# Two of the four value projections of a mixer layer computed in seven half-sized products, as the other two already are, and placed earlier

## The chip, the cores and the metric

The kernel runs on one core of a Trainium2 chip. The core has TensorE (PE: matmuls, with its weight loads listed as PEld), VectorE (DVE), ScalarE (ACT), GpSimd (POOL), SyncE (SP), and 16 DMA engines that move data between DRAM and the on-chip memory SBUF; matmuls write to PSUM, whose banks the other engines empty. The metric is the device time of one execution in microseconds (us); lower is better.

## What is computed

One decoder layer in fp32 on x of 512 x 1024. One projection of x gives queries, keys and values of three attention branches and three gates; the branches are projected, gated and summed, and an MLP follows.

```
proj = x @ w_in
(da_q, da_k, da_v, sb_q, sb_k, sb_v, dl_q, dl_k, dl_v, gates) = split(proj)
o_da = diff_attention(da_q, da_k, da_v, ...)            # 4 heads
o_sb = stick_breaking_attention(sb_q, sb_k, sb_v)       # 8 heads
o_dl = dilated_attention(dl_q, dl_k, dl_v, rel_bias)    # 3 groups x 4 heads
g = sigmoid(gates)
merged = g0 * (o_da @ w_branch_da) + g1 * (o_sb @ w_branch_sb) + g2 * (o_dl @ w_branch_dil)
x = layer_norm(alpha * x + merged @ w_out)
x = layer_norm(alpha * x + square(relu(x @ w_up)) @ w_down + sigmoid(x @ w_ple_gate) * (p @ w_ple))
```

The change concerns the value columns: da_v (512 columns) and dl_v (three groups of 512 columns, dl_v0, dl_v1, dl_v2), each a product of x (512 x 1024) with a 1024 x 512 weight.

## The kernel before

**Products.** Each fp32 product is made of three products of the type fp32r: a number is split into a high part (rounded) and a low part (the rest), and high x high, high x low and low x high are summed in PSUM. A weight chunk is 128 x 1024 (0.5 MB). SyncE loads it into `raw` (a ring of 6), ScalarE casts the high part `wh` (line 264), VectorE subtracts to get the low part `wl` (line 266, "the split"); `wh` and `wl` are rings of 5.

**Items.** The work of TensorE outside the heads is a list of items, each of which fills a PSUM bank and is evacuated. A "T" item makes 128 columns of queries or keys transposed, in 24 matmuls of one chunk. A "V" makes four items (`v_items`, matmuls at 602 to 604, evacuated by the copy at 617), one for each 128 rows of x, 24 matmuls each, all four reading the same four chunks. `value_pair` makes two values together: x and the two weights are treated as 2 x 2 blocks, and seven products of half the depth and half the rows replace eight (Strassen's scheme in Winograd's form). That gives 14 half items of 12 matmuls (570 to 572), two for each of the products 1, 2, 7, 6, 4, 5, 3. Each product reads two chunks of 128 x 1024, so there are 14 chunk splits. Products 1, 2 and 4 read weights as they are; 5 and 6 read sums of weight blocks, `vsum`, made in DRAM; 7 and 3 take the chunk loaded for product 1 or 6 and let GpSimd add one more weight block to it in SBUF after the split (`then_add`, line 178). Products 7, 6, 4 and 5 use sums of blocks of x, the forms u7, u6, u4, u5, made by `mixer_forms` on VectorE and ScalarE (696 to 718); the gates use the same forms later. A product's halves are evacuated by ScalarE copies (577) and by VectorE additions (580 to 590). The halves of a pair alternate between PSUM's mm banks (2) and at banks (6); products 5 and 3 add up in at banks. The attention heads use the at banks too. Values of the dilated branch go to DRAM (`values`, 534) and are read back in the heads' order (`dl_vh`, 542).

**Order.** The list: first items of the stick-breaking branch, then the dilated queries and keys (T), with dl_v0's four items among them, then da_v's four items, then the pair of dl_v1 and dl_v2 (item 31 is its first; `pair_at` holds that number), then groups, gates and the rest. The program is written in the list's order: `pump` issues splits ahead of their items, and with each item the heads in flight advance by one step (8 stick-breaking, 4 dilated, 4 differential heads); a scheduler then arranges the instructions by priority and readiness. The forms start at `pair_at - 6`, the tables of the differential heads at `pair_at + 20`, and from `pair_at + 12` on the splits are ordered behind the heads' last instructions.

**Sums.** The sums of weight blocks (`vsum`, `qsum`, `msum`, `bsum`, `gsum`, `usum`, `dsum`) are made by DMAs that GpSimd issues: a plain copy (1233) or one that adds (1231). They are doled out: each item adds its rate times its size to a credit, and each whole unit of credit issues the next step of a fixed list. Each step waits for an earlier split, so that the steps are spread over the stream. An item without a rate of its own takes it from a table by its number (945).

Of the kernel before, what the change touches and what calls it, by code (L numbers as in the profile page):

```python
# [10 lines left out]
F32 = mybir.dt.float32  # L11
# [24 lines left out]
def main_order():  # L36


    o = [("T", "sb_q", 0), ("T", "sb_k", 0), ("T", "sb_q", 1), ("T", "sb_k", 1), ("V", "sb_v", 0)]
    for j in (2, 3):  # L40
        o += [("T", "sb_q", j), ("T", "sb_k", j)]
    for h in range(2):
        for g in range(3):
            o += [("T", "dl_q", 4 * g + h), ("T", "dl_k", 4 * g + h)]
            if h == 1 and g == 0:
                o += [("V", "dl_v", g)]
    o += [("V", "da_v", 0), ("V", "dl_v", 1), ("V", "dl_v", 2)]
    pairs = [(("dl_q", 4 * g + h), ("dl_k", 4 * g + h)) for h in (2, 3) for g in range(3)]
    groups = [("G", tuple(pairs[2 * i:2 * i + 2]), i) for i in range(3)]
    o += groups[:2]  # L50
    for d in range(4):
        if d == 2:
            o += groups[2:]
        o += [("T", "da_q", d), ("T", "da_k", d)]
    return o


def trunk(tc, a, out):
    nc = tc.nc
    es = ExitStack()  # L60
    with es:
# [23 lines left out]
        def at_bank():  # L85
            return psum.tile([P, 512], F32, name=nm("at"), tag="at", bufs=6)
# [95 lines left out]
        def chained(cs, p, kp, w, sums):  # L182

            if p in (7, 3):
                return then_add(cs[{7: 1, 3: 6}[p]][kp], w[{7: 2, 3: 1}[p]])
            return chunk(sums[p == 6] if p in (5, 6) else w[{1: 0, 2: 1, 4: 3}[p]], 1024)
# [168 lines left out]
        def group_items(gi, pairs):  # L355
# [21 lines left out]
            def add(ps, need, free, run, ev, bank):  # L377
                for p in ps:
                    at = {5: 0, 6: 1, 7: 2, 3: 3}.get(p)
                    cs[p] = [chunk(w[{1: 0, 2: 1, 4: 3}[p]] if at is None else qsum[gi][at], 1024)]  # L380
                item([c for p in free for c in cs[p]], lambda b: run(), lambda b: ev(),
                     need=[c for p in need for c in cs[p]], bank=bank)
                items[-1]["rate"] = 0.5

            def put(*args):
                with tc.high_priority():
# [121 lines left out]
                T["sb_q", 0], T["sb_k", 0] = evac_sides(*ps, scale["sb_q"])  # L508
            item(parts + [cs[k][0] for k in (1, 3, 5, 7)], mm, ev, bank=lambda: (at_bank(), at_bank()))

        vsum = [[dram.tile([P, 1024], F32, name=f"vsum{m}_{i}") for i in range(2)] for m in range(2)]
        def load_xr():

            r = {}
# [27 lines left out]
                nc.gpsimd.dma_start(t.rearrange("p (c d) -> p c d", c=4), rows)  # L542
            return [t.rearrange("p (c d) -> p c d", c=4) for t in ts]

        def value_pair(nv):


            pair_at.append(len(items))
            cs, s, x = {}, {}, {}
            w = [[a["wv"][nv + n, 2 * h + kp].rearrange("p k n -> p (k n)") for n in range(2) for h in range(2)]  # L550
                 for kp in range(2)]

            for p in (1, 2, 7, 6, 4, 5, 3):
                for r in range(2):
                    if not r:
                        cs[p] = [chained(cs, p, kp, w[kp], vsum[kp]) for kp in range(2)]

                    def bank(p=p, r=r):
                        if p == 5:
                            x[r] = at_bank()  # L560
                        return x[r] if p in (5, 3) else at_bank() if r else mm_bank()

                    def mm(ps, p=p, r=r):
                        for k in range(4):
                            c = cs[p][k // 2]
                            n = slice(k % 2 * 512, k % 2 * 512 + 512)
                            q = slice(r * P, r * P + P)
                            h, lo = [t[:, q] for t in xf[p][k]]
                            go, end = k == 0 and p != 3, k == 3 and p != 5
                            nc.tensor.matmul(ps, h, c["h"][:, n], start=go, stop=False, skip_group_check=True)  # L570
                            nc.tensor.matmul(ps, h, c["l"][:, n], start=False, stop=False, skip_group_check=True)
                            nc.tensor.matmul(ps, lo, c["h"][:, n], start=False, stop=end, skip_group_check=True)

                    def ev(ps, p=p, r=r):
                        if p in (1, 7):
                            s[p, r] = slot("dl_v")
                            nc.scalar.copy(s[p, r], ps)
                        elif p == 2:
                            t = slot("dl_v")
                            nc.vector.tensor_add(t, s[1, r], ps)  # L580
                            keep(1, r, t)
                        elif p == 6:
                            nc.vector.tensor_add(s[1, r], s[1, r], ps)
                            nc.vector.tensor_add(s[7, r], s[7, r], s[1, r])
                        elif p == 3:
                            nc.vector.tensor_add(s[1, r], s[1, r], ps)
                            keep(1, 2 + r, s[1, r])
                        else:
                            t = slot("dl_v") if p == 4 else s[7, r]
                            nc.vector.scalar_tensor_tensor(t, s[7, r], -1.0, ps, op0=OP.mult, op1=OP.subtract)  # L590
                            keep(2, r + 2 * (p == 5), t)
                    item(cs[p] if r else [], mm, ev, need=cs[p], bank=bank, size=0.5)
                    items[-1]["rate"] = 0.5

        def v_items(nv, name, g):
            cs = [chunk(a["wv"][nv, c].rearrange("p k n -> p (k n)"), 1024) for c in range(4)]
# [29 lines left out]
            for tt in range(4):  # L626
# [14 lines left out]
                def ev(ps, tt=tt):  # L641
                    if name != "sb_v" or tt:
# [1 line left out]
                first = name == "sb_v" and tt < 2  # L644
                item(cs if tt == 3 else [], mm, ev, need=cs[2 * tt:2 * tt + 2] if first else cs,
                     bank=((lambda: two[0]) if tt else at_bank) if first else None)
                items[-1]["rate"] = 0.0 if name == "da_v" and not tt else 2.4

        nt, nv = 2, 0
        pair_at = []  # L650
# [2 lines left out]
        for kind, name, j in order[2:]:  # L653
            if kind == "T":
                t_item(nt, name, j)
                nt += 1
            elif kind == "G":
                group_items(j, name)
            else:
                if name != "dl_v" or j == 0:  # L660
                    v_items(nv, name, j)
                elif j == 1:
                    value_pair(nv)
                nv += 1


# [53 lines left out]
        def seven(forms, operand, bank_of, done):  # L720

            cs = {}
            for p in (1, 2, 7, 6, 4, 5, 3):
                for r in range(2):
# [20 lines left out]
                    if p == 5:  # L745
                        bank_of.get("sums", set()).add(len(items))
                    item(cs[p] if r else [], mm, ev, need=cs[p], bank=bank, size=0.5)
                    items[-1]["rate"] = 1.0

        msum = [[[dram.tile([P, 1024], F32, name=f"msum{n}_{m}_{i}") for i in range(2)] for m in range(2)]  # L750
                for n in range(3)]
# [190 lines left out]
            item([], mm, ev, size=0.08)  # L942

        for j, it in enumerate(items):
            it.setdefault("rate", 3.0 if j < 12 else 2.8 if j < 24 else 0.0 if j < 27 else 2.1 if j < 46 else 2.7)

        gate_alone(0, 1)
        gate_alone(1, 2)
# [247 lines left out]
        def sum_steps():  # L1196
# [32 lines left out]
            def issue(o, i, plus):  # L1229
                if plus:  # L1230
                    i = nc.gpsimd.dma_start(o, i, accum_op=OP.add, max_dma_last_dim=4096)  # L1231
                else:
# [3 lines left out]
                    mybir.DependencyClass.Sync, mybir.DependencyReason.DATA), reason="spread over the main stream")  # L1236

            w = a["wv"].rearrange("g c p k n -> g c p (k n)")
            todo = deque(two_steps(vsum[m], [w[3 + i // 2, i % 2 * 2 + m] for i in range(4)], True)
                         for m in range(2))  # L1240
            todo.extend(up_steps(qsum[m], a["wq"][m]) for m in range(3))
            for n in range(3):
                todo.extend(two_steps(msum[n][m], a["wgm"][n, m]) for m in range(2))
# [905 lines left out]
                except StopIteration:  # L2149
                    pending.remove(g)  # L2150

        DA_TABS = pair_at[0] + 20
        sum_steps_ = sum_steps()
        credit = 0.0
        forms_at = pair_at[0] - 6
# [2 lines left out]
        for n, it in enumerate(items):  # L2158
# [27 lines left out]
            pump(freed, {1: 3, 3: 0, 4: 0, ple_at: 0, ple_at + 1: 0}.get(n, 1 if n < 10 else 2))  # L2186
            if n == 8:
                tie.clear()
            tied[0] = pair_at[0] + 12 <= n < gated_at
            if n == gated_at:  # L2190
                tie.clear()
            if n == 4:
# [165 lines left out]
```

## Time and profile before

| | |
|---|---|
| median of 3 runs | 1031.75 us (1031.61 to 1031.76) |
| the profiled execution's own time | 1031.94 us |
| its span in the trace | 1030.2 us (1.74 us lie around it) |
| instructions | 15628 |
| DMA | 270.74 MB in 79533 packets |
| granted TensorE clock, mean | 0.998 |

Times in the profile are of one execution. A row of a group reads: line, engine, operation, tile written <- tiles read, shape, count; then either the busy time in all and the mean of one in ns, and the idle time before them with its releaser, or the shortest, median and longest duration in ns with the first and last start in us. "x8" is a count. Matmuls are pipelined, so one lasts longer than the distance to the next.

### The profile page before, as it was taken

The page shows a single profiled execution, that of the slowest core. Times are in us where ns is not written, and L with a number is a line of the kernel's source. Part 1 is how long each engine was busy: PE and PEld are TensorE (multiplying, and loading weights), DVE is VectorE, ACT ScalarE, POOL GpSimd, SP SyncE. Part 2 cuts the span into 40 slices and gives each one's busy share as a digit, 9 for nine tenths or more (in the row PEclk, how much of TensorE's full clock was granted, in tenths as well). Part 3 has the DMA queues.
Part 4 walks back from the last instruction along what each step waited for, and adds up shares of the span by engine and source line. Part 5 has one row for each costly group of instructions (what it writes and reads, how often), then busy time and mean ns, then how long its engine had stood idle before and what let it go on. Part 6 is the DMA issues. An engine that isn't in the chain of part 4 may idle for free.

```text
span 1030.2 us, 15628 instructions
## 1 busy us (share of the span) xinstructions
PE 1019.7 (99%) x5650; PEld 883.5 (86%) x5650; DVE 782.5 (76%) x1393; ACT 607.3 (59%) x1045; POOL 205.0 (20%) x307
## 2 busy tenths in 40 slices
PE   9999999999999999999999999999999999999997
PEld 6888888888998898888888888889999899899886
DVE  6888656677656876886878885798768777777975
ACT  7566556665444565656654743776666556556651
POOL 0323421121323122111122140211121111110001
PEclk9999999999999999999999999999999999999999
DMA  8999997778999889778999995699999999988522
GB/s 311 293 287 296 263 292 248 214 209 220 287 342 258 248 266 247 167 232 206 359 315 266 333 340 170 136 251 350 332 306 315 307 342 335 297 256 277 177 80 82
DMA packets 79533, 270.74 MB, mean 263 GB/s; under 512 B 9720, under 2 KB 12552, under 8 KB 79456
## 3 DMA queue, kind: packets, MB, share of 16 engines
q0 software_dynamic: 36624, 130.89, 50.1%
q1 hardware_dynamic: 42256, 137.95, 36.6%
q8 instruction: 44, 0.72, 0.3%
q10 hardware_dynamic: 576, 0.92, 0.2%
q14 instruction: 33, 0.27, 0.1%
HBM read 262.35 MB, written 112.22 MB: 364 GB/s over the span
## 4 chain that ended last, share of the span: by engine, by line
PE 91%; DVE 4%; ACT 2%; DMA 2%; issue 1%; DVEq 0%; ACTq 0%
PE mm L89 9%; PE mm L90 9%; PE mm L91 9%; PE at L1414 4%; PE at L1415 4%; PE at L1416 4%; PE at L737 2%; PE at L735 2%; PE at L736 2%; PE mm L604 2%; PE mm L602 2%; PE mm L603 2%; PE at L91 2%; PE at L90 2%; PE at L89 2%; DMA raw<-in_wb_dram 2%
## 5 line engine op out<-in xcount | busy, mean ns | idle before, releaser
L266 DVE TENSOR_TENSOR wl<-raw,wh 128x1024 fp32r<-128x1024 f32 x268 | 322.7, 1214 | 113.1 <-ACT wh L264 112.0
L264 ACT CAST wh<-raw 128x1024 fp32r<-128x1024 f32 x268 | 277.6, 1042 | 208.0 <-PE mm L90 102.5
L89 PE MATMUL mm<-xhT,wh 128*128 128x512 f32 (+1 forms) x254 | 95.5, 376 | 0.0
L91 PE MATMUL mm<-xhT,wl 128*128 128x512 f32 (+1 forms) x254 | 94.3, 371 | 0.0
L90 PE MATMUL mm<-xlT,wh 128*128 128x512 f32 (+1 forms) x254 | 94.1, 370 | 0.0
L1414 PE MATMUL at<-wh,hh 128*128 128x512 f32 x188 | 73.7, 392 | 0.0
L1415 PE MATMUL at<-wl,hh 128*128 128x512 f32 x188 | 73.7, 392 | 0.0
L1416 PE MATMUL at<-wh,hl 128*128 128x512 f32 x188 | 73.1, 389 | 0.0
L89 PE MATMUL mm<-x1hT,wh 128*128 128x256 f32 x256 | 72.8, 284 | 0.0
L90 PE MATMUL mm<-x1lT,wh 128*128 128x256 f32 x256 | 72.4, 283 | 0.0
L91 PE MATMUL mm<-x1hT,wl 128*128 128x256 f32 x256 | 72.4, 283 | 0.0
L91 PEld LDWEIGHTS mm<-xhT,wl 128*128 128x128 f32 x254 | 47.8, 188 | 8.3
L89 PEld LDWEIGHTS mm<-xhT,wh 128*128 128x128 f32 x254 | 47.9, 188 | 7.7 <-PE mm L604 0.2
L90 PEld LDWEIGHTS mm<-xlT,wh 128*128 128x128 f32 x254 | 47.9, 189 | 7.5
L89 PEld LDWEIGHTS mm<-x1hT,wh 128*128 128x128 f32 x256 | 48.9, 191 | 1.9
L90 PEld LDWEIGHTS mm<-x1lT,wh 128*128 128x128 f32 x256 | 48.9, 191 | 1.5
L91 PEld LDWEIGHTS mm<-x1hT,wl 128*128 128x128 f32 x256 | 48.9, 191 | 0.0
L1231 POOL DMA_DIRECT2D usum<-in_wu_dram x32 | 29.2, 914 | 92.7 <-DVE wl L266 50.4
L1231 POOL DMA_DIRECT2D dsum<-in_wd_dram x28 | 24.8, 887 | 107.6 <-DVE wl L266 42.2
L1416 PEld LDWEIGHTS at<-wh,hl 128*128 128x128 f32 x188 | 35.3, 188 | 7.7
L1414 PEld LDWEIGHTS at<-wh,hh 128*128 128x128 f32 x188 | 35.5, 189 | 6.2
L1415 PEld LDWEIGHTS at<-wl,hh 128*128 128x128 f32 x188 | 35.5, 189 | 5.7
(671 smaller groups left out, 2853.0 us busy)
## 6 DMA issues: line engine op xcount, KB each, us to landing
usum<-in_wu_dram POOLq DMA_DIRECT2D x48, 512.0 KB, 9.1
dsum<-in_wd_dram POOLq DMA_DIRECT2D x42, 512.0 KB, 9.5
raw<-usum SPq DMA_DIRECT2D x32, 512.0 KB, 8.0
raw<-dsum SPq DMA_DIRECT2D x28, 512.0 KB, 6.9
raw<-in_wt_dram SPq DMA_DIRECT2D x26, 512.0 KB, 7.9
raw<-in_wd_dram SPq DMA_DIRECT2D x25, 512.0 KB, 6.5
raw<-in_wu_dram SPq DMA_DIRECT2D x24, 512.0 KB, 7.9
raw<-in_wv_dram SPq DMA_DIRECT2D x18, 512.0 KB, 7.4
```

What stands on the lines that cost most here:

```text
L89: nc.tensor.matmul(ps, wh, xh, start=start, stop=False, skip_group_check=True)
L90: nc.tensor.matmul(ps, wh, xl, start=False, stop=False, skip_group_check=True)
L91: nc.tensor.matmul(ps, wl, xh, start=False, stop=stop, skip_group_check=True)
L264: i = nc.scalar.copy(h, raw)
L266: i = nc.vector.tensor_sub(lo, raw, h.bitcast(F32))
L602: nc.tensor.matmul(ps, x1, c["h"][:, s], start=k == 0, stop=False)
L603: nc.tensor.matmul(ps, x1, c["l"][:, s], start=False, stop=False)
L604: nc.tensor.matmul(ps, x2, c["h"][:, s], start=False, stop=k == 7)
L1231: i = nc.gpsimd.dma_start(o, i, accum_op=OP.add, max_dma_last_dim=4096)
L1414: nc.tensor.matmul(ps, h[:, q], c["h"][:, s], start=go, stop=False, skip_group_check=True)
L1415: nc.tensor.matmul(ps, h[:, q], c["l"][:, s], start=False, stop=False, skip_group_check=True)
L1416: nc.tensor.matmul(ps, lo[:, q], c["h"][:, s], start=False, stop=end, skip_group_check=True)
```

## The change

dl_v0 and da_v are made by `value_pair` too. The 12 T items of the dilated queries and keys in the list no longer have dl_v0 among them; behind the last of them stand two pairs, dl_v0 with da_v (items 23 to 36), then dl_v1 with dl_v2 (items 37 to 50). There are two sets of `vsum`, and the first pair's are made first; `have` sends da_v to its own place instead of to DRAM. The first pair's products 5 and 3 add up in mm banks, the second's in at banks as before. The forms start six items ahead of the first pair, at item 17 where it was 25; the differential heads' tables and the ties of the splits are counted from the second pair. The rates are set anew: 1.5 and 0.7 for the halves of the two pairs (0.5), 0.7 for the groups' halves (0.5), 1.2 for the gates' (1.0), and a new table.

```diff
@@ -42,9 +42,7 @@
             o += [("T", "dl_q", 4 * g + h), ("T", "dl_k", 4 * g + h)]
-            if h == 1 and g == 0:
-                o += [("V", "dl_v", g)]
-    o += [("V", "da_v", 0), ("V", "dl_v", 1), ("V", "dl_v", 2)]
+    o += [("V", "dl_v", 0), ("V", "da_v", 0), ("V", "dl_v", 1), ("V", "dl_v", 2)]
@@ -380,7 +378,7 @@
-                items[-1]["rate"] = 0.5
+                items[-1]["rate"] = 0.7
@@ -508,7 +506,8 @@
-        vsum = [[dram.tile([P, 1024], F32, name=f"vsum{m}_{i}") for i in range(2)] for m in range(2)]
+        vsum = [[[dram.tile([P, 1024], F32, name=f"vsum{n}_{m}_{i}") for i in range(2)] for m in range(2)]
+                for n in range(2)]
@@ -542,9 +541,16 @@
-        def value_pair(nv):
+        def value_pair(nv, names):
+
+            def have(n, tt, t):
+                name, g = names[n]
+                if name == "dl_v":
+                    keep(g, tt, t)
+                else:
+                    V[name, g, tt] = t
+
+            sums = vsum[len(pair_at)]
@@ -553,11 +559,11 @@
-                        cs[p] = [chained(cs, p, kp, w[kp], vsum[kp]) for kp in range(2)]
+                        cs[p] = [chained(cs, p, kp, w[kp], sums[kp]) for kp in range(2)]
...
-                            x[r] = at_bank()
+                            x[r] = mm_bank() if sums is vsum[0] else at_bank()
@@ -578,19 +584,19 @@
-                            keep(1, r, t)
+                            have(0, r, t)
...
-                            keep(1, 2 + r, s[1, r])
+                            have(0, 2 + r, s[1, r])
...
-                            keep(2, r + 2 * (p == 5), t)
+                            have(1, r + 2 * (p == 5), t)
                     item(cs[p] if r else [], mm, ev, need=cs[p], bank=bank, size=0.5)
-                    items[-1]["rate"] = 0.5
+                    items[-1]["rate"] = 0.7 if len(pair_at) > 1 else 1.5
@@ -644,7 +650,7 @@
-                items[-1]["rate"] = 0.0 if name == "da_v" and not tt else 2.4
+                items[-1]["rate"] = 2.4
@@ -657,10 +663,10 @@
-                if name != "dl_v" or j == 0:
+                if name == "sb_v":
                     v_items(nv, name, j)
-                elif j == 1:
-                    value_pair(nv)
+                elif nv % 2:
+                    value_pair(nv, [v[1:] for v in order if v[0] == "V"][nv:nv + 2])
@@ -745,7 +751,7 @@
-                    items[-1]["rate"] = 1.0
+                    items[-1]["rate"] = 1.2
@@ -942,7 +948,7 @@
-            it.setdefault("rate", 3.0 if j < 12 else 2.8 if j < 24 else 0.0 if j < 27 else 2.1 if j < 46 else 2.7)
+            it.setdefault("rate", 3.0 if j < 12 else 2.8 if j < 16 else 0.0 if j < 20 else 2.3 if j < 52 else 3.2)
@@ -1236,8 +1242,8 @@
-            todo = deque(two_steps(vsum[m], [w[3 + i // 2, i % 2 * 2 + m] for i in range(4)], True)
-                         for m in range(2))
+            todo = deque(two_steps(vsum[n][m], [w[1 + 2 * n + i // 2, i % 2 * 2 + m] for i in range(4)], True)
+                         for n in range(2) for m in range(2))
@@ -2149,7 +2155,7 @@
-        DA_TABS = pair_at[0] + 20
+        DA_TABS = pair_at[1] + 20
@@ -2186,7 +2192,7 @@
-            tied[0] = pair_at[0] + 12 <= n < gated_at
+            tied[0] = pair_at[1] + 12 <= n < gated_at
```

Lines of the changed kernel are shifted: the pair's matmuls stand at 576 to 578, their evacuations at 583 to 596, the cast and the split at 262 and 264, the sums' DMAs at 1237 (adding) and 1239.

On TensorE, before, the pair begins behind the last of da_v's four items (`mm_2296`); `xhT` and `xlT` are the high and low part of x, the number behind a name tells the tiles apart:

```order
L602 MATMUL mm_2296<-wh_2023,xhT 128x512
L603 MATMUL mm_2296<-wl_2024,xhT 128x512
L604 MATMUL mm_2296<-wh_2023,xlT 128x512
L570 MATMUL mm_2363<-wh_2095,xhT 128x512
L571 MATMUL mm_2363<-wl_2096,xhT 128x512
L572 MATMUL mm_2363<-wh_2095,xlT 128x512
```

Now, at the start of the first pair, its first half (`mm_1896`) stands right behind matmuls of a stick-breaking head (1842 and 1847), whose operands VectorE has just made:

```order
L1842 MATMUL at_1602<-sph_1783,tri_r 128x512
L1842 MATMUL at_1602<-spl_1784,tri_r 128x512
L1847 MATMUL at_1602<-smh_1706,ones_r 128x384
L1847 MATMUL at_1602<-sml_1707,ones_r 128x384
L576 MATMUL mm_1896<-wh_1572,xhT 128x512
L577 MATMUL mm_1896<-wl_1573,xhT 128x512
L578 MATMUL mm_1896<-wh_1572,xlT 128x512
```

So a pair now starts among the stick-breaking heads, where before it started behind da_v.

On VectorE, before, this is one stretch of the stick-breaking heads beside T items. The tiles `e`, `spl`, `sm`, `smp` and `al` are the heads', `wl` is a split:

```order
L1807 SCALAR_TENSOR_TENSOR e_1845<-at_1832,e_1845 128x512
L1811 TENSOR_TENSOR spl_1851<-e_1845,sph_1850 128x512
L1820 TENSOR_TENSOR sm_1854<-e_1845 128x256
L1822 CAST smp_1856<-sm_1854 128x256
L1823 TENSOR_TENSOR smp_1856<-sm_1854,smp_1856 128x256
L1851 TENSOR_TENSOR al_1879<-a_1876,ah_1878 128x384
L1851 TENSOR_TENSOR al_1889<-a_1886,ah_1888 128x512
L266 TENSOR_TENSOR wl_1905<-raw_1520,wh_1904 128x1024
L1807 SCALAR_TENSOR_TENSOR e_1912<-at_1831,e_1912 128x384
```

And now, the same steps of a head beside the first pair:

```order
L1813 SCALAR_TENSOR_TENSOR e_1882<-at_1869,e_1882 128x512
L264 TENSOR_TENSOR wl_1946<-raw_1253,wh_1945 128x1024
L1817 TENSOR_TENSOR spl_1888<-e_1882,sph_1887 128x512
L1826 TENSOR_TENSOR sm_1891<-e_1882 128x256
L264 TENSOR_TENSOR wl_1956<-raw_1457,wh_1955 128x1024
L1828 CAST smp_1893<-sm_1891 128x256
L1829 TENSOR_TENSOR smp_1893<-sm_1891,smp_1893 128x256
L1857 TENSOR_TENSOR al_1919<-a_1916,ah_1918 128x384
L1857 TENSOR_TENSOR al_1929<-a_1926,ah_1928 128x512
L1813 SCALAR_TENSOR_TENSOR e_1963<-at_1868,e_1963 128x384
```

Between one `e` and the next there was one split, and now there are two.

On GpSimd, the first sums to be issued were, before, one pair's `vsum` and then `qsum`:

```order
L1233 DMA vsum_0_84<-in_wv_dram 128x1024
L1233 DMA vsum_0_86<-in_wv_dram 128x1024
L1233 DMA qsum_0_72<-in_wq_dram 128x1024
L1233 DMA qsum_0_76<-in_wq_dram 128x1024
L1231 DMA vsum_0_84<-in_wv_dram 128x1024
L1231 DMA vsum_0_86<-in_wv_dram 128x1024
```

And now both pairs' `vsum`:

```order
L1239 DMA vsum_0_0_84<-in_wv_dram 128x1024
L1239 DMA vsum_1_0_86<-in_wv_dram 128x1024
L1239 DMA vsum_0_0_88<-in_wv_dram 128x1024
L1239 DMA vsum_1_0_90<-in_wv_dram 128x1024
L1237 DMA vsum_0_0_84<-in_wv_dram 128x1024
L1237 DMA vsum_1_0_86<-in_wv_dram 128x1024
```

The `qsum` steps have moved behind them.

## The prediction

> **What bounds the kernel now.** I read the page's busy shares first, with its chain that ended last, since they say whether one engine sets the end or several in turn.
>
> ```profile
> span 1030.2 us, 15628 instructions
> PE 1019.7 (99%) x5650; PEld 883.5 (86%) x5650; DVE 782.5 (76%) x1393; ACT 607.3 (59%) x1045; POOL 205.0 (20%) x307
> PE 91%; DVE 4%; ACT 2%; DMA 2%; issue 1%; DVEq 0%; ACTq 0%
> ```
>
> TensorE is busy for 99% of the span and carries 91% of the chain. A share is a mean over stages, so the windows come next (the stretch in us; then its length, and each engine's busy us with its instructions; granted clock, DMA share, GB/s).
>
> ```profile
> 0.00:25.00 25.00, 23.73 (x100) 17.26 (x101) 17.61 (x31) 18.12 (x28) 1.69 (x10) 1.00 0.89 319
> 25.00:1000.00 975.00, 972.84 (x5439) 846.74 (x5438) 746.58 (x1322) 582.45 (x1003) 198.23 (x290) 1.00 0.89 267
> 1000.00:1030.20 30.20, 23.16 (x115) 19.52 (x113) 18.30 (x40) 6.76 (x17) 5.04 (x7) 0.93 0.19 70
> ```
>
> From 25 to 1000 us TensorE lacks only 2.16 us in 975, and the granted clock is 1.00. The idle time lies in the lead-in (1.3 us) and in the tail (7.0 us), neither of which the change touches. So a matmul taken out of the middle is worth its issue interval, as long as nothing else comes late there. The view of TensorE's waits says what does come late (line waited at, releaser, total us, times, longest):
>
> ```profile
> PE at L1611 <- DVE zero L1608: 1.2, 1, 1.2
> PE at L1928 <- ACT scr L1933: 0.7, 1, 0.7
> PE at L2069 <- DVE L L2045: 0.5, 2, 0.4
> PE mm L570 <- DVE da_v L617: 0.3, 1, 0.3
> ```
>
> Only the fourth belongs to code that changes: the first product of the value pair waits for a PSUM bank that VectorE empties of da_v. No row names a weight load.
>
> **What the change removes.** dl_v0 and da_v are now two times four items of 24 matmuls, 192. As a pair they are 14 half items of 12, 168. Twenty-four matmuls of 128x512 go. The spacing of such matmuls is read from their starts (start, us of one, engine, line), 27 intervals between these two:
>
> ```profile
> 155.14 0.39 PE L602 MATMUL mm<-wh,xhT 128*128 128x512 f32 x1
> ...
> 161.27 0.39 PE L602 MATMUL mm<-wh,xhT 128*128 128x512 f32 x1
> ```
>
> 6.13 us / 27 = 0.227 us, where one lasts 0.39 because they are pipelined. 24 x 0.227 = **5.45 us** off TensorE.
>
> The weight load of such a matmul is shorter (ns min/median/max):
>
> ```profile
> L602 PEld LDWEIGHTS mm<-wh,xhT x88: 187/188/188, 31.5 to 219.9; 128*128 128x128 f32 x88
> ```
>
> The Trainium skill, "Perfetto Trace Analysis", section "Identifying the Most-Contended Engine", says that matmul busy time is a poor measure of TensorE's headroom, and wants the share of LDWEIGHTS instead. That would be 86% here, with room left, and the removed work would be 24 x 0.188 = 4.5 us. The spacing of the starts speaks against it: TensorE issues nothing closer than 0.227 us in a stretch without waits, so I count by that.
>
> **What it adds.** The pair reads 14 weight chunks where the eight items read 8, so ScalarE gets six more casts and VectorE six more splits.
>
> ```profile
> L264 ACT CAST wh<-raw x268: 612/1049/1102, 15.3 to 1000.0; 128x1024 fp32r<-128x1024 f32 x131, 128x512 fp32r<-128x512 f32 x3
> L266 DVE TENSOR_TENSOR wl<-raw,wh x268: 684/1223/1236, 16.4 to 1001.1; 128x1024 fp32r<-128x1024 f32 x131, 128x512 fp32r<-128x512 f32 x3
> L617 DVE COPY dl_v<-mm x4: 683/685/692, 146.8 to 166.5; 128x512 f32<-128x512 f32 x4
> L590 DVE SCALAR_TENSOR_TENSOR dl_v<-dl_v,at x3: 672/674/680, 257.7 to 260.3; 128x512 f32<-128x512 f32 x3
> L577 ACT COPY dl_v<-mm x2: 587/588/589, 224.3 to 238.1; 128x512 f32<-128x512 f32 x2
> ```
>
> VectorE: 6 x 1.223 = 7.3 us, and 12 evacuations of a pair in place of 8 copies, 4 x 0.68 = 2.7: +10.1 us. ScalarE: 6 x 1.049 = 6.3 and four copies, 4 x 0.588 = 2.4: +8.6 us. Over the whole span both have room (76% and 59%). What counts is the stage where the first pair now lies, beside the stick-breaking heads:
>
> ```profile
> 25.00:70.00 45.00, 45.00 (x214) 36.90 (x213) 37.65 (x76) 28.05 (x49) 12.41 (x18) 1.00 1.02 275
> 160.00:205.00 45.00, 45.00 (x219) 37.34 (x217) 31.32 (x50) 28.88 (x46) 7.29 (x11) 1.00 0.79 240
> 219.00:265.00 46.00, 45.72 (x216) 37.96 (x215) 35.47 (x80) 24.57 (x43) 11.55 (x17) 1.00 0.86 233
> ```
>
> 160 to 205 is the stick-breaking stage without a pair, 219 to 265 the pair of today. From the same stretch, by line:
>
> ```profile
> L266 DVE TENSOR_TENSOR wl<-raw,wh 128x1024 fp32r<-128x1024 f32 x8 | 9.8, 1224 | 5.7 <-ACT wh L264 5.5
> L617 DVE COPY dl_v<-mm 128x512 f32<-128x512 f32 x2 | 1.4, 688 | 0.9 <-PE mm L604 0.9
> L347 DVE COPY dl_k<-mm 128x512 f32<-128x512 f32 x2 | 1.4, 688 | 0.0
> L704 DVE TENSOR_TENSOR xr<-xr,xr 128x512 f32<-128x512 f32 x2 | 1.4, 683 | 0.0
> ```
>
> Take from 31.3 its eight splits (9.8) and four copies (2.8), add 14 splits (17.1) and 12 evacuations (8.2): 44.0 us of VectorE in 45, an upper bound. The forms of x stand in that stretch as four groups like the last row (L704, L709, L710, L714; 4 x 1.4 = 5.6 us), and they are still made six items ahead of the first pair, so most now fall before the stage: 38.4 us, 85%. For ScalarE the same step gives 28.9 + 6 x 1.05 + 2.4 = 37.6 us, 84%. The nearest row with so full a VectorE is 25 to 70 us: 37.65 busy of 45, and TensorE 45.00 of 45. The pair of today, at 35.47, costs TensorE 0.28 us. The added work is therefore mostly covered. Its cost is bounded by 0 (the first row) and by a bank wait of today's size, 0.28 us, in each of the 14 halves, 3.9 us. The pair of today shows one wait in 14 halves; I take **1.0 us**, some four such waits, because the stage is fuller and because in the new order the halves of different products are cut up and woven among the heads' matmuls. Where the cover is gone, an item waits for its split or its bank, and everything behind it on TensorE stands still.
>
> **What moves.** The second pair is today's pair, beside the dilated heads as now, with the same work; the tables and turns of the differential heads are now counted from it and keep their distance. The forms of x come eight items earlier: 5.6 us of VectorE go into a stretch where it now idles 13.7 us of 45 (the row of 160 to 205); that idle time hides them, and without it they would cost up to 5.6, which is the step from 38.4 to 44.0 above.
>
> **Sums and loads.** The first pair needs eight more steps of the sums, on GpSimd's queue, and four more transfers that add into a loaded chunk (ns of issuing one; then us from issue to landing):
>
> ```profile
> L1231 POOL DMA_DIRECT2D vsum<-in_wv_dram x4: 805/819/885, 31.1 to 55.0; - x4
> L178 POOL DMA_DIRECT2D raw<-in_wv_dram x4: 843/888/904, 196.6 to 235.1; - x4
>   ACT wh L264: 3.3, 2
> raw<-in_wv_dram POOLq DMA_DIRECT2D x4, 512.0 KB, 8.3
> ```
>
> 12 x 0.82 = 9.8 us of a queue that is 20% busy. TensorE waits for none of this issuing by itself. The eight steps take the places of the qsum steps, which are issued later; the higher rates then catch up. Of the pair's 14 chunks four are made by adding, so SyncE reads ten where it read eight. All of it is 8 + 4 + 2 = 14 transfers of 0.5 MB, 7.3 MB more on 271, while the queues have 0.79 to 0.89 of the time in these stages. No TensorE wait in the old profile names a sum, and the groups that read qsum follow the pairs in the program, so I cost the sums at nothing: the stretch between a sum's last step and its load hides them. The transfers that chase a load could cost what ScalarE waited for them (the row "ACT wh": 3.3 us in two waits, over the 20 such transfers of the kernel), and this is a rival below. Below nothing: the 0.28 us of da_v may go, and part of the 2.16 us idle between 25 and 1000; at most about 1 us of it lies near the moved items.
>
> **The sum.** The profiled execution took 1031.94 us, 0.19 more than the median. 1031.94 - 5.45 + 1.0 = 1027.49; against the median that is 1031.75 - 4.45 = **1027.3 us**.
>
> **Rivals.**
> *Each half waits.* If VectorE's queue, served in order, hands every half its bank late, the 14 halves give back 3.9 us: 1031.75 - 5.45 + 3.9 = 1030.2. For it: splits, evacuations and the heads' e, spl, al steps share one queue, and two splits now stand where one stood. Against it: at 84% busy (25 to 70) TensorE lost nothing.
>
> *VectorE becomes the bound of the first pair (slower).* Take its work at the upper bound, 44.0 us, and idle time that it can't give up as in the stage of today's pair, 46.0 - 35.5 = 10.5 us: 54.5 us for TensorE's 45, so +9.5: 1031.75 - 5.45 + 9.5 = 1035.8. It decides as soon as VectorE's work and its forced idle time together exceed the 45 us that TensorE needs there; at my 38.4 us of work that takes 6.6 us of forced idle time, at 44.0 only 1.0. Against it: from 25 to 70 the idle time was 7.35 us, so 10.5 isn't forced; and most forms lie ahead.
>
> *The added transfers land late.* Eight such chunks now, four of them in the fuller stage. If each of these makes TensorE wait as ScalarE did, 3.3 / 2 = 1.65 us, 6.6 us are given back: 1032.9.
>
> *The change doesn't pay at the end.* The matmuls surely go, but the time is lost to later loads because all sums after the first are shifted: about 1031.7. Against it: no load wait in TensorE's rows, and a lead-in and tail that don't move.
>
> *GpSimd and VectorE shut each other out.* If each of 12 more issues held VectorE for its 0.82 us and this reached TensorE, +9.8: 1036.1. The split's longest time, 1236 ns against a median of 1223 in 268 while 300 instructions ran on GpSimd, speaks against it. The Trainium skill, "SBUF — State Buffer", section "SBUF: two separate sides", has the rule: the two share a pair of ports under an exclusive lock, and a DMA issued from GpSimd may find it taken. The longest split leaves 13 ns for it.
>
> **How the numbers follow.** Forecast 0.72 (waits of 0 to 3.3 us); each half waits 0.12; VectorE bound 0.05; late transfers 0.03; no pay 0.04; the lock 0.04. A measurement of this kernel tells about 0.2%, 2.06 us, from no change: faster is below 1029.69. So faster 0.72; within it 0.12 + 0.03 + 0.04 = 0.19; slower 0.05 + 0.04 = 0.09. The range goes from 1025.4 (no wait, 1026.3, and some 0.9 us of old waits gone) to 1030.6 (the wait of each half, 1030.2, and a little), which leaves out 0.16.
>
> **What would show it.** TensorE: 24 matmuls fewer, 5.4 us less busy, the stage of the first pair some 5 us shorter. Waits of TensorE at the pair's first line for dl_v or an evacuation, between 160 and 210 us: about 1 us in all if right, near 4 if each half waits. VectorE near 38 us in that stage's 45 with TensorE full; if TensorE falls there below 43 of 45, VectorE is the bound. No wait for raw or a sum; if ScalarE's cast waits for raw and TensorE stands behind it, the transfers are late. A longest split well above 1236 ns would show the lock. What would make the forecast wrong is a wait that these rows can't show because its place doesn't exist yet: two halves that need the same bank out of turn.

## The result, and the profile after

The changed kernel takes **1061.97 us** (4 runs, 1058.97 to 1065.73) where the kernel before, timed beside it, takes 1031.76: a ratio of 1.0293, interval 1.0253 to 1.0333. It is 30 us slower, and its runs lie 7 us apart where those of before lie 1 us apart. The profiled execution took 1059.67 us, with a span of 1058.0.

The page of the changed kernel, in the lines that were read before:

```profile
span 1058.0 us, 15640 instructions
PE 1022.8 (97%) x5626; PEld 883.5 (84%) x5626; DVE 789.9 (75%) x1403; ACT 614.3 (58%) x1055; POOL 212.7 (20%) x319
PE 85%; DMA 7%; DVE 4%; ACT 2%; issue 1%; POOL 0%; DVEq 0%; SPq 0%; ACTq 0%; POOLq 0%
```

The 24 matmuls are gone (5650 to 5626). TensorE's idle time has grown from 1030.2 - 1019.7 = 10.5 us to 1058.0 - 1022.8 = 35.2. Its busy time has grown too, by 3.1 us, with fewer matmuls: some of them ran at a lower clock. DMA has risen from 2% to 7% of the chain. TensorE's waits say where (line waited at, releaser, total us, times, longest):

```profile
PE at L1868 <- DVE al L1857: 13.7, 1, 13.7
PE mm L833 <- DVE graw L786: 3.8, 1, 3.8
PE at L576 <- DVE dl_v L589: 2.2, 1, 2.2
PE mm L87 <- DVE dl_k L345: 2.1, 1, 2.1
PE at L1617 <- DVE zero L1614: 1.2, 1, 1.2
PE mm L576 <- ACT wh L262: 1.1, 1, 1.1
PE at L1842 <- ACT sph L1816: 0.9, 1, 0.9
```

The largest names VectorE (`al`, a stick-breaking head's tile). VectorE's own timeline shows that it was the messenger (start, us, engine, line, operation, in brackets the idle time before it and its end):

```profile
147.98 0.69 DVE L1817 TENSOR_TENSOR spl<-e,sph 128x512 fp32r<-128x512 f32 x1
148.58 0.42 DVE L1826 TENSOR_TENSOR sm<-e 128x256 f32<-128x256 f32 x1
162.69 0.69 DVE L710 TENSOR_TENSOR xr<-xr,xr 128x512 f32<-128x512 f32 x1 [13.69 <-DMA xr<-in_xT_dram]
```

Line 710 is the first operation of the forms of x. It waits for `xr`, the 2 MB of x that SyncE loads for them in eight transfers of 256 KB, and the heads' work stands behind it in VectorE's queue. The view of this tile, before and then after (a DMA row's duration is that of issuing one):

```profile
L519 SPq DMA_DIRECT2D xr<-in_xT_dram x8: 385/420/864, 183.5 to 187.1; - x8
DMA to landing us min/median/max: 4.0/5.7/6.4
```

```profile
L518 SPq DMA_DIRECT2D xr<-in_xT_dram x8: 413/468/3530, 128.4 to 136.8; - x8
DMA to landing us min/median/max: 4.1/20.1/29.4
```

The same bytes land up to 29.4 us after issue instead of 6.4. What GpSimd issued beside them is different. Its timeline from 168 to 190 us before, and from 128 us on after:

```profile
168.53 1.04 POOL L1233 DMA_DIRECT2D msum<-in_wgm_dram  x2
181.20 0.57 POOL L672 DMA_DIRECT2D oT<-oT  x1 [11.63 <-DVE oT L1869]
188.77 0.53 POOL L1233 DMA_DIRECT2D bsum<-in_wbq_dram  x1 [7.00 <-DVE wl L266]
```

```profile
128.31 0.92 POOL L1237 DMA_DIRECT2D qsum<-in_wq_dram  x1 [13.95 <-DVE wl L264]
128.89 1.21 POOL L1237 DMA_DIRECT2D msum<-in_wgm_dram  x1
129.45 1.19 POOL L1239 DMA_DIRECT2D qsum<-qsum  x1
135.07 1.04 POOL L1239 DMA_DIRECT2D qsum<-qsum  x2 [4.43 <-DVE wl L264]
...
148.92 1.19 POOL L1237 DMA_DIRECT2D qsum<-in_wq_dram  x1
149.45 1.19 POOL L1239 DMA_DIRECT2D msum<-in_wgm_dram  x1
```

Before, GpSimd issued no step of the sums from 169.6 us to 188.8, and `xr` went out at 183.5. Now it is idle for 13.95 us, resumes in the very moment in which `xr` goes out, and issues nine steps of 0.5 MB in 21 us. Both kernels have a gap of four items without steps (rate 0.0) around the start of the forms. But by the code a step waits for the oldest entry of a list of four, `marks`, into which each split puts itself. Beside T items, with one split each, the steps that follow the gap (item 20) so wait for the split for which `xr` (item 17) waits: the gap is there in the list of items and not in time. In the old kernel the gap ends beside V items. Each evacuation of such an item puts itself twice into `marks`, so that its oldest entry is a recent one:

```
i = nc.vector.tensor_copy(t, ps)
marks.append(getattr(i, "ins", i))
marks.append(getattr(i, "ins", i))
```

The waits of the old kernel show such a mark at work (`POOL bsum L1233 <- DVE da_v L617: 16.0, 2, 10.0`: two steps waited 16.0 us for copies of da_v). With the V items of this stretch the change takes these marks away; nothing in the pair replaces them.

The windows from 150 to 180 us show what the wait costs beside itself (granted clock, DMA share and GB/s last):

```profile
150.00:156.00 6.00, 3.76 (x17) 2.79 (x15) 0.00 (x0) 1.05 (x1) 0.64 (x2) 1.00 1.06 225
156.00:164.00 8.00, 0.00 (x0) 0.00 (x0) 1.31 (x3) 0.59 (x1) 0.00 (x0) 0.62 0.81 241
164.00:172.00 8.00, 4.55 (x14) 3.83 (x15) 8.00 (x14) 2.08 (x5) 0.00 (x0) 0.52 0.20 64
172.00:180.00 8.00, 5.87 (x34) 4.95 (x32) 5.05 (x10) 5.21 (x9) 0.54 (x1) 1.00 0.18 57
```

The granted clock falls to a half during the wait (at 158 us) and is back at 1.00 from 172 us on, so that the first matmuls after the wait, from 167.4 us, run for some 4 us at half the rate. The profile's account is then: idle time + 24.7 us, busy time - 5.45 for the matmuls and + 8.5 for those at the lower clock (worked out as the rest), together the 27.8 us between the two spans.

### The profile page after: what moved, and what is told of

It is laid out like the page before. It is cut to its first block, busy times and chain, and to the rows that moved or that the text cites. A ratio compares the mean times of both kernels' runs of the same rounds, so it can differ in the third digit from the quotient of the medians.

```text
span 1058.0 us, 15640 instructions
## 1 busy us (share of the span) xinstructions
PE 1022.8 (97%) x5626; PEld 883.5 (84%) x5626; DVE 789.9 (75%) x1403; ACT 614.3 (58%) x1055; POOL 212.7 (20%) x319
## 4 chain that ended last, share of the span: by engine, by line
PE 85%; DMA 7%; DVE 4%; ACT 2%; issue 1%; POOL 0%; DVEq 0%; SPq 0%; ACTq 0%; POOLq 0%
PE mm L87 9%; PE mm L88 9%; PE mm L89 8%; PE at L1420 4%; PE at L1421 4%; PE at L1422 4%; DMA xr<-in_xT_dram 3%; DMA raw<-in_wb_dram 2%; PE at L741 2%; PE at L743 2%; PE at L742 2%; PE at L89 2%; PE at L88 2%; PE at L87 2%; PE at L1033 1%; PE at L1031 1%
## 5 line engine op out<-in xcount | busy, mean ns | idle before, releaser
L264 DVE TENSOR_TENSOR wl<-raw,wh 128x1024 fp32r<-128x1024 f32 (+1 forms) x274 | 329.9, 1213 | 128.2 <-ACT wh L262 127.0
L262 ACT CAST wh<-raw 128x1024 fp32r<-128x1024 f32 (+1 forms) x274 | 283.7, 1042 | 221.9 <-PE mm L88 107.1
L1237 POOL DMA_DIRECT2D usum<-in_wu_dram x32 | 29.4, 930 | 124.9 <-DVE wl L264 54.8
```

The costliest lines, as they stand in the source:

```text
L262: i = nc.scalar.copy(h, raw)
L264: i = nc.vector.tensor_sub(lo, raw, h.bitcast(F32))
```

## The experiments

The theories. **A**: transfers that something waits for (first `xr`) share the DMA engines with bursts of steps, land late, hold an in-order queue, and TensorE behind it. **B**: the second pair's own work on VectorE and ScalarE is the bound, and the wait for `xr` only fills slack. **C**: 7.3 MB more are too much, and moving a transfer only moves the wait. Each ratio is against the kernel before, timed beside it (1031.86 to 1032.11 us).

**Steps later, loads earlier, the old kernel with early forms, longer pieces.** The first edit lets the steps issued with items 16 to 29 wait for the newest split (the changed part of the line; `now[0]` is the item's number):

```diff
-marks[0].name
+marks[-1 if 16 <= now[0] < 30 else 0].name
```

> The changed kernel, but the steps of the sums that are issued with items 16 to 29 wait for the newest split instead of the split four before it. Theory A (the 2 MB of x for the forms, eight transfers named xr, share the DMA engines with a burst of steps, land up to 29.4 us after issue, hold VectorE's queue 13.7 us and TensorE behind it): nine steps leave the stretch 128 to 150 us, xr lands within 8 us as before, the 13.7 us and the 2.1 us after it go, and with them the stretch of half clock (about 3 us): 1062 - 19 = about 1043, the losses near 210 to 225 and 527 us staying. Theory B (the extra pair's own work on VectorE and ScalarE beside the stick-breaking heads is the bound, and the wait for xr only fills slack): at least 1055. Theory C (the 7.3 MB more are too much for the DMA engines, a transfer moved only shifts the wait): about 1060.

Measured: 1047.76 us, 1.0142 (1.0112 to 1.0173); `xr` lands 5.9 us after issue, and no wait for it is left. The second issues `xr` three items earlier and leaves VectorE's work in its place:

```diff
-        forms_at = pair_at[0] - 6
+        forms_at = pair_at[0] - 9
...
-            for _ in range(6):
+            for _ in range(9):
```

> The changed kernel, but the eight loads xr are issued three items earlier, in the stretch where GpSimd issues no step (112 to 128 us); VectorE's work on them stays where it is. Theory A: xr lands before 128 us, no wait at VectorE's first form, about 1043. Theory B: at least 1055. Theory C: about 1060.

Measured: 1044.59 us, 1.0119 (1.0101 to 1.0138); landing 5.7 us. The third makes the converse test in the kernel before:

```diff
-        forms_at = pair_at[0] - 6
+        forms_at = pair_at[0] - 14
```

> The kernel before, with only the forms (their loads and VectorE's work) started eight items earlier, at item 17 as in the changed kernel; no second pair, no further sums, the old rates. Theory A: xr now falls among the steps that the old rates issue from 126 to 142 us and lands some 20 us after issue; VectorE's queue waits for it by 5 to 14 us and TensorE behind it: 1038 to 1050. Theories B and C: 1031.8, since the pair and its 7.3 MB are not there.

Measured: 1048.18 us, 1.0152 (1.0134 to 1.0171): the old kernel, with its old rates and without a second pair, loses 16 us by the early forms alone. Its view of `xr`:

```profile
L519 SPq DMA_DIRECT2D xr<-in_xT_dram x8: 409/502/2903, 128.8 to 138.7; - x8
its engine sat idle before it (us, times) until:
  DMA xr<-in_xT_dram: 13.3, 1
...
DMA to landing us min/median/max: 10.6/16.8/21.3
```

VectorE stands still for 13.3 us, as in the changed kernel. The fourth reads the same bytes at the same time, from a copy of x laid out so that they come in pieces of 2 KB instead of 1 KB (again the changed part of the line):

```diff
-xt[:, 4 * h + 2 * kp:4 * h + 2 * kp + 2, 256 * th:256 * th + 256]
+a["xq"][:, 4 * h + 2 * th + kp].rearrange("p (k t) -> p k t", k=2)
```

> The changed kernel, but x for the forms is read from a copy laid out so that each row of a transfer is 2 KB in one piece, where it is two pieces of 1 KB; same bytes, same time of issue, same steps beside it. If what delays xr is the count of its pieces (the engines take them in turn with the 4 KB pieces of the sums), it lands in about half the time, 15 us instead of 29, and most of the 13.7 us goes: about 1046. If only bytes count: 1060 to 1062.

Measured: 1051.93 us, 1.019 (1.0166 to 1.0214):

```profile
L518 SPq DMA_DIRECT2D xr<-in_xq_dram x8: 333/424/546, 129.0 to 133.0; - x8
its engine sat idle before it (us, times) until:
  DMA xr<-in_xq_dram: 2.3, 1
...
DMA to landing us min/median/max: 4.3/12.9/19.8
```

Beside the same steps `xr` lands a third sooner (19.8 for 29.4 at the longest), and VectorE waits 2.3 us instead of 13.7. The time lies between the two that were expected, so the size of the pieces is part of the delay and not all of it. All four agree with A for the largest wait, and e3 excludes B and C for it: neither the pair nor its bytes are in that kernel. What they don't explain is the rest. By A e1 and e2 should have come to about 1043. e2 did; e1 lies 5 us above, with a wait of 4.2 us at 234 us and one of 2.6 at 596 that the changed kernel doesn't have. And 1043 is still 11 us above before.

**The remaining waits, and the rates.** In e2_xr_early TensorE still waits 4.2 us for a bank at 510 us (its releaser `graw`; the chunks of wb land 14 to 22 us after issue, among eight transfers of `oT` and the steps: six from 478 to 501 us, where the old kernel issues five beside the same loads) and 3.4 us near 196 us, where ScalarE waits for a slot of SBUF that a write of values still holds:

```profile
196.73 0.58 ACT L583 COPY dl_v<-mm 128x512 f32<-128x512 f32 x1 [2.84 <-DMA values<-dl_v]
198.13 0.58 ACT L583 COPY dl_v<-at 128x512 f32<-128x512 f32 x1 [0.81 <-DMA oT<-oT]
```

The next edits go on from e2_xr_early (rates, old -> new).

```diff
 e5: first pair 1.5 -> 0.8; MLP 0.63 -> 0.67
 e6: table's last 3.2 -> 2.0; gates 1.2 -> 0.9; MLP 0.63 -> 0.76
 e7: both; MLP 0.63 -> 0.80
```

> As e2_xr_early, and the first pair's halves give the sums a rate of 0.8 where the change set 1.5; the steps that this puts off are made up later (0.67 for 0.63 in the MLP). In e2_xr_early TensorE still loses about 5 us around 190 to 200 us, where ScalarE waits 2.8 us for a slot that a late write of values holds. If the write is late because of the steps beside it (theory A for this place too): that loss goes to under 1.5 us, and the time falls by 3 to 5 us to about 1040. If the pair's own work is the bound there (theory B): unchanged, 1043 to 1046.

Measured: 1043.79 us (1037.95 to 1046.95), 1.0092 (1.0061 to 1.0123). The profile has 1.7 + 2.3 us of waits near 197 and 232 us where e2 had 3.4 + 1.9, the wait at 510 is gone, and new ones stand elsewhere (3.5 us at a differential head, 2.6 in two waits near 607 us). By its time alone it lies where B put it (1043 to 1046), by the wait near 197 halfway: inconclusive.

> As e2_xr_early, with the change's higher rates after the pairs taken back: 2.0 for 3.2 in the table's last entry, 0.9 for 1.2 at the gates, made up in the MLP (0.76 for 0.63). In e2_xr_early TensorE waits 4.2 us at 510 us for a bank, because VectorE and ScalarE wait for the chunk of wb that lands 21 us after issue, with two more steps beside it than before. Theory A: that wait falls under 0.5 us and the half clock after it goes, 6 us: about 1038. Theory B has nothing to say here; if the later first-pair stages cause it: unchanged.

Measured: 1052.65 us, 1.0199 (1.0183 to 1.0215): a miss. The wait at 510 us did go. But the steps put off come too late for the end:

```profile
974.76 1.04 ACT L262 CAST wh<-raw 128x1024 fp32r<-128x1024 f32 x1 [15.28 <-DMA raw<-dsum]
```

SyncE can't read `dsum` before its last step has landed, and TensorE waits 8.4 us there.

> Both edits of e5_pair_rate and e6_late_rates on e2_xr_early. Theory A: the losses add up, so the time is that of e2_xr_early less both, 1033 to 1035, with one wait of 1.6 us near 154 us left over; without any wait the matmuls taken out would give 1027. Theory B: 1038 or more.

Measured: 1057.92 us, 1.0253 (1.0226 to 1.028), with 10.8 us in that place and 6.5 more in five waits for ScalarE's evacuations of the MLP: a miss.

**No steps at all.** To measure what the pair costs when nothing lands late, both kernels were run without the sums. In the changed kernel, and likewise in the one before:

```diff
-                next(sum_steps_, None)
+                pass
```

and the seven kinds of sums are replaced by plain weight blocks that are read in their place.

> The changed kernel without any step of the sums; where a sum is read, a plain weight block of the same size is read. It leaves out the making of all sums of weight blocks, so its output differs; TensorE, VectorE and ScalarE have the same work. Theory A: without the steps nothing lands late, the second pair costs what the forecast gave it, and the time lies 4 to 6 us below that of e10_before_no_sums, near 1026. Theory B (the pair's own work on VectorE and ScalarE): the waits beside the stick-breaking heads stay, and the time is at or above e10_before_no_sums.

> The kernel before with the same work left out: no steps of the sums, plain blocks read in their place. The old kernel hardly waits for transfers: 1030 to 1031.8 by both theories. It is the base for e9_after_no_sums.

Measured: 1029.90 us against 1032.18, each from 10 runs (1029.29 to 1031.39, and 1032.00 to 1032.69); against the kernel before, 0.9981 (0.9971 to 0.999) and 1.0001 (0.9991 to 1.001). So the change is worth 2.3 us when no step is in the way, about half of what was expected, and the sums cost the kernel before nothing. `xr` lands within 6.1 us there, issued at item 17. TensorE's waits in e9_after_no_sums, and its window:

```profile
PE mm L93 <- DVE dl_k L351: 2.1, 1, 2.1
PE at L1623 <- DVE zero L1620: 1.2, 1, 1.2
PE at L1848 <- ACT sph L1822: 0.9, 1, 0.9
PE at L1940 <- ACT scr L1945: 0.7, 1, 0.7
160.00:205.00 45.00, 41.98 (x199) 34.05 (x198) 34.67 (x54) 34.13 (x54) 3.38 (x5) 1.00 0.42 123
```

The first and the third are new: 3.0 us, all that TensorE lacks of the 45. The first ends at 164.8 us, 7 us ahead of the pair's first matmul (171.9): a T item needs a bank that VectorE empties (into `dl_k`) only behind work on the forms. Those operations run from 149.5 us on, and from 147.4 to 164.6 VectorE stands idle for 1.0 us of 17.2. The third, 0.9 us, is a stick-breaking head's, beside the pair. So B's kind of wait, behind VectorE's and ScalarE's work, makes up 3 us, and the larger part comes from the forms and not from the pair. No run took the forms alone away, so that part is read from the timeline. The other 32 us (1061.97 - 1029.90) are the steps' doing.

**Dealing the steps out otherwise.** All go on from e2_xr_early and keep the number of steps; the sums' rates are

```diff
 e8:  first pair from item 28 on 0.8; groups 0.95; table's last 3.65; gates' last twelve halves 0.6
 e11: as e8, groups 0.7, table's last 4.0, MLP 0.66
 e12: as e11, the forms in every second item
 e13: as e11, table's last 3.2, MLP 0.71
 e14: as e13, first pair from item 28 on 0.0, second pair 1.3
```

> As e2_xr_early, with the steps of the sums moved between items and none of them left for the MLP: the first pair's halves from item 28 on give 0.8 for 1.5 and the groups 0.95 for 0.7; the second and third gate's halves beside the loads of oT and wb give 0.6 for 1.2 and the last entry of the table 3.65 for 3.2. Theory A (late transfers among bursts of steps): the waits near 195 and 510 us shrink as in e5_pair_rate and e6_late_rates and no new wait comes in the MLP: 1034 to 1038. If the steps only find another victim wherever they go: 1041 to 1046.

Measured: 1043.91 us, 1.0117 (1.0102 to 1.0132), a miss. The waits at 196 and 510 us are down to 1.2 and nothing, and one of 12.6 us has come at 372 us. Its chain, from ScalarE's and from GpSimd's timeline:

```profile
370.51 0.38 ACT L406 ACTIVATE gs<-at 128x256 f32<-128x256 f32 x1 [13.92 <-DMA oT<-oT]
```

```profile
351.23 0.82 POOL L1239 DMA_DIRECT2D gsum<-in_wg_dram  x1 [0.69 <-DMA gsum<-in_wg_dram]
...
364.16 0.54 POOL L1241 DMA_DIRECT2D gsum<-gsum  x1 [5.32 <-DMA gsum<-in_wg_dram]
364.69 0.59 POOL L678 DMA_DIRECT2D oT<-oT  x1
```

A write of `oT`, which ScalarE's next tile needs out of its slot, stands in GpSimd's queue behind a step that waits for the step before it.

> As e8_spread, with the groups' rate back at 0.7 (0.95 there), and the steps that this puts off made up at the last entry of the table (4.0) and a little in the MLP (0.66 for 0.63). In e8_spread one wait was left, 12.6 us near 372 us, where ScalarE waits for a slot that a write of oT holds; that write stands in GpSimd's queue behind a step of gsum, which waits for the step before it. Theory A: that place is free of steps again, the 13.3 us go and nothing else changes: 1030 to 1032. If steps always find another late transfer: 1038 or more.

Measured: 1039.69 us, 1.0078 (1.0066 to 1.009), a miss: 7.7 us are left in that place.

> As e11_spread_groups_back, and the four forms of x are made in every second item instead of in every item, the first three items earlier. What is left of the waits in the stage of the first pair without late transfers is 1.6 us, where ScalarE casts forms ahead of an evacuation (2.1 us in e9_after_no_sums). With the forms spaced out it goes: 1 to 2 us below e11_spread_groups_back, 1029 to 1030. If it is the splits and evacuations of the pair itself: same as e11_spread_groups_back.

Measured: 1041.99 us, 1.0093 (1.0074 to 1.0112): no gain. The wait of 1.6 us for ScalarE's evacuation near 155 us became two, of 1.2 and 0.7.

> As e11_spread_groups_back, with the table's last entry back at the change's 3.2 and the steps made up in the MLP (0.71). In e11_spread_groups_back 7.7 us were lost near 370 us behind a step of gsum that the rate of 4.0 had brought there. Theory A: that wait and the half clock after it go, 8 us: 1031 to 1033, about the kernel before; what stays is some 4 us near 190 us. If the steps always find another late transfer: 1037 or more.

Measured: 1038.63 us (1035.10 to 1044.20), 1.0062 (1.0041 to 1.0083), a miss. The wait near 364 us is down to 1.3 us; a new one of 1.7 us, with half clock behind it, stands near 671 us.

> As e13_table_back, and the first pair's halves from item 28 on give no steps, which the second pair makes up (1.3 for 0.7). If the 4 us near 190 us (ScalarE and VectorE waiting for slots that writes of values hold) come from steps beside those writes, they go: 1028 to 1029, faster than the kernel before. If they come from the pair's own loads and the slots: as e13_table_back.

Measured: 1042.71 us, 1.0102 (1.008 to 1.0123). The waits near 196 us are gone, so steps caused them, but near 364 us there are 6.8 again: a miss in the total. e8, e11 and e13 came out where their expectations put them if the steps always find another late transfer. That is the second half of theory C, so C isn't excluded for what is left: whether it is the order of the steps or the 7.3 MB more that keeps these runs above before is open. No dealing out that was tried beats the kernel before; that there is none isn't shown.

## Why the prediction was wrong

1. **The step that failed** stands under "What moves": "The forms of x come eight items earlier: 5.6 us of VectorE go into a stretch where it now idles 13.7 us of 45 (the row of 160 to 205); that idle time hides them". It left out the forms' eight loads, 2 MB, which move with the operations. These now meet the steps; VectorE's queue waits 13.7 us for them (that this equals the idle time counted there is chance). e1 and e2 take this away (14 and 17 us), e3 brings it into the old kernel (16 us). The operations were half counted, too: the old kernel's view of `xr` has, beside the eight of 0.68 us that make the 5.6, eight more on VectorE that split the forms, of which these are the first and the last two:

```profile
L294 DVE TENSOR_TENSOR u7l<-xr,u7h x2: 674/675/676, 207.7 to 208.3; 128x512 fp32r<-128x512 f32 x2
L294 DVE TENSOR_TENSOR u5l<-xr,u5h x2: 683/684/686, 218.2 to 219.9; 128x512 fp32r<-128x512 f32 x2
```

   So about 11 us of VectorE moved, and without any step in the way TensorE waits 2.1 us behind them (e9).
2. **The sums at nothing** was the second: "I cost the sums at nothing: the stretch between a sum's last step and its load hides them". That holds for the sums as data: none of TensorE's waits in the changed kernel points to a sum that came late. It doesn't hold for them as traffic: with and without steps the changed kernel differs by 32 us, the old one by nothing measurable. The text looked at how full the DMA engines are on average (0.79 to 0.89), and not at which transfer that something waits for would meet a burst.
3. **The sum itself** comes out at half: without steps the change gains 1032.18 - 1029.90 = 2.3 us where 4.45 were forecast. The term for the pair's waits, 1.0 us, fits in size the 0.9 measured beside the pair, though not in kind: it was meant as some four waits of halves for their banks, and it is one wait of a head. What is missing are the 2.1 us of the forms, the same step as in 1.
4. **The rivals.** "The added transfers land late" was the nearest, though with the wrong transfers and a fifth of the price (6.6 us of 32): none of TensorE's waits in the changed kernel leads back to a load to which a block is added. "VectorE becomes the bound" had as its sign a TensorE below 43 us of 45, and e9_after_no_sums has 41.98. But VectorE is busy 34.67 us there, less than the 38 forecast, and is full only in the 17 us ahead of the pair: the mechanism holds for some 2 us, not for the 9.5 of that rival. "Each half waits" isn't seen: the halves wait three times in the changed kernel (2.2, 1.1 and 0.8 us), and in e9 not at all. That GpSimd's issues hold VectorE isn't seen either. Of the changed kernel's splits:

```profile
L264 DVE TENSOR_TENSOR wl<-raw,wh x274: 683/1220/1227, 15.7 to 1029.0; 128x1024 fp32r<-128x1024 f32 x134, 128x512 fp32r<-128x512 f32 x3
```

   The longest is 7 ns over the median, with 12 more transfers issued by GpSimd.
5. **The range** took its upper end from a wait of 0.28 us. A stall of 13.7 us behind a load that is late by 23 us was in no row of the stage, but the old profile had rows that warned of it: `oT` by SyncE's queue at a median of 16.0 us to landing and the chunks of wb at 15.7 are transfers that meet steps already, in a kernel that waits 0.2 us behind them. e10_before_no_sums shows it: without steps the two land at a median of 9.0 and 8.0 us.

## What to carry to other kernels

When code that computes is moved, list the loads it issues and ask what is on the DMA engines at the new place; an in-order engine that reaches such a load early stops everything queued behind it. Background traffic that is doled out by waits on other work (here on the oldest of four marks) changes its timing when that work changes, even where its rates are meant to keep a gap. To price a change in such a kernel, run both versions without the background traffic: it separates what the change is worth (2.3 us) from what the background traffic costs it (32 us).

## What the runs showed of the hardware

- TensorE's granted clock drops to about 0.5 in a wait of 13.7 us, and also in one of 3.8 us (near 530 us, in the changed kernel), and stays there for the first 4 to 5 us of work behind it; after the wait of 2.1 us, in e9_after_no_sums, its mean over the window stays 1.00. The Trainium skill, "TensorE: Matmul & The Clock Gate", section "Part 1: The HAM clock gate (the "warmup" mystery)", says that the clock is halved after an idle window of some 3.4 us, and these three agree with it. The changed kernel has a place that doesn't fit so simply: from 219.7 to 225.4 us four matmuls run between waits of 1.1, 0.8 and 2.2 us, and the clock is at 0.5 from 223 us, before the longest of the three is over. Here short waits close together went with half the clock, too.
- Loads in 1 KB pieces lose against transfers of the sums on the same engines: `xr` landed in 29.4 us at the longest, in 2 KB pieces in 19.8, with the same bytes. The Trainium skill, "DMA: Bandwidth & Descriptors", section "Queues, rings and completion order", says that an engine takes its queues in turn, packet by packet; that the longer pieces gain by such turns fits, though no run here varied the turns themselves.
